# Five seven-product pairs per feed-forward unit, with the copies, sums and residual adds around them re-ordered

## The chip, the cores and the metric

The kernel runs on one core of one Trainium2 chip. The metric is the device time of one execution, in microseconds. Engines are named as in the profile: PE (TensorE) multiplies, DVE (VectorE) and ACT (ScalarE) work element by element, POOL (GpSimd) does a little of both and issues some transfers, SP (SyncE) issues the weight loads. TensorE writes to eight PSUM banks of 128 x 512 float32; everything else lies in SBUF.

## The reference

An encoder of two layers over 256 tokens, width 2048. Layer 0 mixes with grouped-query attention, layer 1 with a gated recurrence; after each mixer comes a feed-forward part, which is where the change lies:

```python
x = x + mixer(rms_norm(x, norm_mix[i]))
x = x + swiglu(rms_norm(x, norm_ffn[i]), w_gate[i], w_up[i], w_down[i])

def swiglu(h, w_gate, w_up, w_down):
    return (jax.nn.silu(h @ w_gate) * (h @ w_up)) @ w_down
```

w_gate and w_up are 2048 x 5632, w_down is 5632 x 2048. All inputs are float32.

## The kernel before

**Precision.** Each float32 operand is split into a high part (rounded to float32r, by a cast on ScalarE) and a low part (what is left, a subtraction on VectorE). One product of a 128 x 128 block of activations and a 128 x 512 block of weights is three matmuls: high x high, low x high, high x low (`product`, L291 to L297).

**Weights.** They stream in halves of 512 KB (1024 values per partition), in the order in which they are used. `load_half` (L119) issues the load on SP, casts on ACT (L127) and subtracts on DVE (L128). Raw halves have five buffers, split ones seven (`parts`, L108). `behind` (L114) chains all casts in program order, and all subtractions and sums of weights ("rest") in another chain, so on their engines these keep the order of the program. TensorE's order is the program's. Everything else on ACT, DVE and POOL is placed by a scheduler that goes through the program with a timeline of its own; within an engine instructions run in the order so fixed, and an instruction that waits holds back those behind it. `follow` adds one more constraint of order between two instructions.

**A feed-forward unit.** The 5632 hidden features are taken as 11 units of 512. A unit (L714) computes gate and up for its features and both halves of the tokens (a = 0, 1), over the 16 blocks of the input width in eight pairs c = 0 to 7. Four accumulators c11, c21 (gate) and c12, c22 (up) collect in PSUM. A plain pair takes two halves of weights and eight products, 24 matmuls. A seven-product pair treats the pair of blocks as a 2 x 2 matrix product by Strassen's scheme in Winograd's form and needs seven products, 21 matmuls. It pays for this with sums: `load_seven` (L136) forms four sums of weight blocks on DVE (L151, 128 x 512 each) and splits them too (L145 on ACT, L148 on DVE); the sums of activations ("forms") are made once per layer while the norm is turned (`form`, L425), one per pair that any unit computes in this way. Four more accumulators, m1, p5, p7, p6, serve these pairs. `SEVEN` (L30) names the pairs; `FEWER` (L31) gives fewer to units 0 to 2.

The seven products of a pair run in this order:

```python
(m1, a11, "b11"), (c11, a12, "b21"), (c12, n4, "b22"), (p5, n1, "t1"),
(p7, n3, "t3"), (p6, n2, "t2"), (c21, a22, "t4"),
```

**The end of a unit.** After its last seven-product pair: m1 is copied on ACT (L741), p6, p5, p7 and p5 again are added or subtracted on DVE (L742 to L745). After pair 7: c11 and c21 are added on DVE (L747), Silu on ACT, c12 and c22 subtracted from (L750), the products taken (L751). Then the 128 x 1024 result is transposed: DVE transposes 32 x 32 blocks (L376), sixteen ACT copies put them in place (L383), and the result is split again (L753, L754).

**Order of the work.** `ffn_plan` (L178): units 0 and 1, then each further unit followed by two of the four "down" groups of the part before it (one group: 512 output columns, 8 blocks of hidden features, four halves of weights, 48 matmuls), unit 10 without any; at the end the last part of 12 blocks (`groups`, L323). The four m1, p5, p7, p6 banks and the down groups' banks come from one pool of four ("pm"); c11 to c22 and the last part's banks from another pool of four ("acc"). Each down group's two banks are added to the residual x_tm (in SBUF) by `add_residual` (L314, the add is L317, on DVE).

Of the kernel before, what the change touches and what calls it, by code (L numbers as in the profile page):

```python
# [12 lines left out]
F32 = mybir.dt.float32  # L13
F32R = mybir.dt.float32r
AF = mybir.ActivationFunctionType
ALU = mybir.AluOpType
AX = mybir.AxisListType

P = 128
S = 256  # L20
# [6 lines left out]
DFF = 5632  # L27
PARTS = [8, 8, 8, 8, 12]
UNIT = 4
SEVEN = (0, 1, 3, 5)  # L30
FEWER = {0: (0, 3, 5), 1: (1, 5), 2: (1, 5)}  # L31
HALF = 8
CHUNK = HALF * P
WIDE = 512
# [38 lines left out]
def trunk(ctx, tc, w, out):  # L73
    nc = tc.nc
    act, dve, pool, pe, sync = nc.scalar, nc.vector, nc.gpsimd, nc.tensor, nc.sync
# [15 lines left out]
    def tmp(tag, shape=(P, S), dt=F32, bufs=2):  # L91
        pl = tp if tag in COMMON else scope[-1]
        return pl.tile(list(shape), dt, tag=tag, name=nm(tag), bufs=bufs)
# [4 lines left out]
    def follow(i, j):  # L98
        tc.add_manual_dep(
            i.ins, j.ins.name,  # L100
            mybir.DependencyInfo(mybir.DependencyClass.NoSync, mybir.DependencyReason.DATA),
            reason="order",
        )


    ring, held, ft = [0], [], []

    def parts(shape):  # L108
        n = ring[0] = (ring[0] + 1) % (RING + MORE)
# [4 lines left out]
    def behind(key, i):  # L114
        if key in newest:
            follow(i, newest[key])
        newest[key] = i

    def load_half(src, pieces=1, then=None):  # L119
        raw = wp.tile([P, CHUNK], F32, tag="raw", name=nm("raw"), bufs=RING)  # L120
# [15 lines left out]
    def load_seven(srcs):  # L136
        raw = [wp.tile([P, 2, WIDE], F32, tag="raw", name=nm("raw"), bufs=RING) for _ in range(2)]
        for r, src in zip(raw, srcs):
            sync.dma_start(out=r, in_=src)
        (b11, b21), (b12, b22) = ([r[:, j, :] for j in range(2)] for r in raw)  # L140
        got = {}

        def two(src, names):
            hi, lo = parts([P, 2, WIDE]) if len(names) > 1 else [tmp(t, (P, 1, WIDE), F32R) for t in ("ohi", "olo")]
            behind("cast", act.copy(hi, src))  # L145
            for j, name in enumerate(names):
                got[name] = hi[:, j, :], lo[:, j, :]
            return lambda: behind("rest", dve.tensor_tensor(lo, src, hi[:].bitcast(F32), ALU.subtract))  # L148

        def add(o, x, y):  # L150
            behind("rest", dve.tensor_tensor(o, x, y, ALU.add))  # L151

        sums = [tmp("ws", (P, 2, WIDE)) for _ in range(2)]
        (t1, t3), (t2, t4) = ([t[:, j, :] for j in range(2)] for t in sums)
        two(raw[0], ("b11", "b21"))()
        add(t1, b11, b12)
        add(t3, b12, b22)
        two(raw[1][:, 1:, :], ("b22",))()
        first = two(sums[0], ("t1", "t3"))
        add(t2, t1, b22)  # L160
        add(t4, t2, b21)
        second = two(sums[1], ("t2", "t4"))
        first()
        second()
        return got
# [21 lines left out]
    def ffn_order(l):  # L187
        seq = []
        for what, i in ffn_plan():
# [3 lines left out]
            both = [(w[f"w_gate{l}"][i, c], w[f"w_up{l}"][i, c]) for c in range(KT // 2)]  # L193
            seq += sum(([b] if c in (FEWER.get(i, SEVEN)) else list(b) for c, b in enumerate(both)), [])
        return seq + out_order(w[f"w_down{l}_{len(PARTS) - 1}"], UNIT // 2)
# [112 lines left out]
    def wide_project(xs, total, bank=new_acc):  # L308
        accs = [bank() for _ in range(2)]
        for k0 in range(0, total, 2):  # L310
            wide(accs, xs, k0, total)
        return accs

    def add_residual(g, accs, norm, store=False):  # L314
        for a in range(2):
            o = x_tm[:, a, g * WIDE : (g + 1) * WIDE]
            dve.tensor_tensor(o, o, accs[a], ALU.add)  # L317
            if store:
                sync.dma_start(out=out[:, a, g * WIDE : (g + 1) * WIDE], in_=o)
        if norm is not None:  # L320
            norm.add(g)
# [30 lines left out]
    x_tm = cst.tile([P, 2, D], F32, tag="x", name="x")  # L352
# [17 lines left out]
        return pk[:, o : o + 1]  # L370


    def turn_blocks(src, engines, own=None):
        turned = tmp("one", (P, 2, WIDE), bufs=1)
        own = tmp("two", (P, 2, WIDE), bufs=1) if own is None else own
        dve.transpose(turned, src)  # L376
        t = own.rearrange("p a (b c) -> p (a b) c", c=S)
        for i in range(4):
            of = turned[32 * i : 32 * i + 32].rearrange("p a (k j c) -> p k a j c", k=4, j=4)
            for j in range(4):  # L380
                to = t[32 * j : 32 * j + 32].rearrange("p k (a i c) -> p k a i c", a=2, i=4)
                eng = engines[(4 * i + j) % len(engines)]
                (eng.copy if eng is act else eng.tensor_copy)(to[:, :, :, i, :], of[:, :, :, j, :])  # L383
        return t

    class Norm:
# [30 lines left out]
        def turn(self, g, engines):  # L417
# [3 lines left out]
            for i in range(2):  # L421
                if self.g[0] == "norm_ffn" and 2 * g + i in SEVEN:
                    self.form(2 * g + i, t[:, 2 * i : 2 * i + 2, :])

        def form(self, c, src):  # L425
# [4 lines left out]
            for i, x, y, op in (  # L430
# [3 lines left out]
                pool.tensor_tensor(t[:, i, :], x, y, op)  # L434
            hi, lo = (tmp(f"f{n}", (P, 4, P), F32R, bufs=len(SEVEN)) for n in "hl")
            act.copy(hi, t)
# [227 lines left out]
    def act_four():  # L664
        return xp.tile([P, UNIT, 2 * S], F32R, tag="act", name=nm("act"), bufs=4)
# [44 lines left out]
    def ffn(norm, nxt):  # L710
        def bank():
            return ps_m.tile([P, 2 * S], F32, tag="pm", name=nm("pm"))

        def unit(seven):  # L714
            xs, r = norm.xs, [norm.r[:, a : a + 1] for a in range(2)]
            m1, p5, p7, p6 = (bank() for _ in range(4))
            c11, c21, c12, c22 = (new_acc() for _ in range(4))
            new = [m1, p5, p7, p6, c11, c21, c12, c22]

            def fresh(o):  # L720
                n = len(new)
                new[:] = [b for b in new if b is not o]
                return len(new) < n

            for c in range(KT // 2):
                if c not in seven:
                    for pair in ((c11, c21), (c12, c22)):
                        wide(pair, xs, 2 * c, KT, [fresh(o) for o in pair])
                    continue
                wt, end = half(), c == seven[-1]  # L730
                n1, n3, n2, n4 = norm.forms[c]
                a11, a12, a22 = block(xs, 2 * c, 0), block(xs, 2 * c + 1, 0), block(xs, 2 * c + 1, 1)
                for o, x, y in (
                    (m1, a11, "b11"), (c11, a12, "b21"), (c12, n4, "b22"), (p5, n1, "t1"),
                    (p7, n3, "t3"), (p6, n2, "t2"), (c21, a22, "t4"),
                ):
                    product(o, x, wt[y], fresh(o), end and any(o is m for m in (m1, p5, p7, p6)))
                if end:
                    one, h = (tmp(n, (P, 2, WIDE), bufs=1) for n in ("one", "two"))
                    (base, u), (v, x) = ([t[:, a, :] for a in range(2)] for t in (one, h))  # L740
                    act.copy(base, m1)  # L741
                    dve.tensor_tensor(u, base, p6, ALU.add)  # L742
                    dve.tensor_tensor(v, u, p5, ALU.subtract)
                    dve.tensor_tensor(u, u, p7, ALU.add)
                    dve.tensor_tensor(x, u, p5, ALU.subtract)  # L745
            for o, y, b in ((base, base, c11), (u, u, c21)):
                dve.tensor_tensor(o, y, b, ALU.add)  # L747
            for a, (o, y, b) in enumerate(((base, v, c12), (u, x, c22))):
                table_act(o, o, AF.Silu, scale=r[a])
                dve.tensor_tensor(y, b, y, ALU.subtract)  # L750
                dve.scalar_tensor_tensor(y, y, r[a], o, ALU.mult, ALU.mult)  # L751
            t, ht = act_four(), turn_blocks(h, (act,), h)
            act.copy(t[:, :, :S], ht)  # L753
            dve.tensor_tensor(t[:, :, S:], ht, t[:, :, :S].bitcast(F32), ALU.subtract)  # L754
            return [t[:, k, :] for k in range(UNIT)]

        hid = [[] for _ in PARTS]
        ends = np.cumsum(PARTS) // UNIT
        for what, i in ffn_plan():
            if what == "unit":  # L760
                hid[int(np.searchsorted(ends, i, "right"))] += unit(FEWER.get(i, SEVEN))
            else:
                add_residual(i[1], wide_project(hid[i[0]], PARTS[i[0]], bank), None)
        if nxt is not None:
            ln_exp_tables()
        groups(hid[-1], PARTS[-1], PARTS[-1] - UNIT, lambda: None, partial(add_residual, norm=nxt, store=nxt is None))
        scope.pop()
        ft.pop().close()
# [216 lines left out]
```

## Time and profile before

| What | Value |
|---|---|
| three runs, us | 1986.05 to 1988.11, median 1986.53 |
| the profiled execution's own time, us | 1986.03 |
| its span, first to last instruction, us | 1984.2 |
| TensorE's granted clock, mean | 0.999 |
| busy: PE / DVE / ACT / POOL, us | 1970.6 / 1674.4 / 1333.5 / 267.6 |
| feed-forward, units 3 and 4 (423.4 to 548.6), us | 125.2 |

Rows of groups read: line, engine, operation, output <- inputs, shapes, count | busy us, mean ns of one | idle time of the engine before them and what ended it. Rows of the timeline read: start us, duration us, engine, line, operation, operands, count (an "x2" row covers two instructions back to back), and in brackets the engine's idle time before it with what released it. Rows of waits read: who waited <- for whom: us in total, times, longest. Rows of one tile's instructions give the shortest, median and longest duration in ns. Rows of a window give its length and, for each engine, busy us and instructions; then clock, DMA share and GB/s. A matmul's duration is modelled and overlaps with the next one's, so its price is the distance from start to start.

### The profile page before, as it was taken

To read this page: it belongs to the slowest core of one execution; us is meant where nothing else is said; L and a number is where in the kernel's file an instruction comes from. 1 tells how busy PE (TensorE), PEld (TensorE's weight loads), DVE (VectorE), ACT (ScalarE), POOL (GpSimd) and SP (SyncE) were. 2 spreads that over 40 slices of the span, in tenths; PEclk is the share of its full clock that TensorE was granted. 3 is DMA by queue.
4 is the path that set the end of the run, shared out by engine and by line. 5 is a ranking of instruction groups with operands and counts; after the bars stand their busy time and mean duration, and the time that the engine had idled before them with its cause. 6 is when DMAs were issued, how large, how long until landed. Compare 5 with 4: busy or idle time off the path is not lost.

```text
span 1984.2 us, 27870 instructions
## 1 busy us (share of the span) xinstructions
PE 1970.6 (99%) x9892; PEld 1677.0 (85%) x9892; DVE 1674.4 (84%) x2204; ACT 1333.5 (67%) x2081; POOL 267.6 (13%) x323
## 2 busy tenths in 40 slices
PE   9999999999999999999999999999999999999999
PEld 8888887888888888888999998878888888888887
DVE  7878699889899898987788986897898898988983
ACT  7677577666656666567688886867666666666662
POOL 0443150000000000000456540510000000000000
PEclk9999999999999999999999999999999999999999
DMA  8534646646675556656566555555576456655663
GB/s 315 165 126 132 208 150 223 217 166 208 193 242 196 174 200 205 233 193 203 189 194 184 190 157 185 197 188 194 181 234 213 169 203 201 234 202 168 202 219 132
DMA packets 108571, 386.06 MB, mean 195 GB/s; under 512 B 12176, under 2 KB 12432, under 8 KB 108304
## 3 DMA queue, kind: packets, MB, share of 16 engines
q1 hardware_dynamic: 108288, 384.26, 58.5%
q8 instruction: 78, 1.28, 0.3%
q14 instruction: 61, 0.50, 0.1%
q10 hardware_dynamic: 144, 0.02, 0.0%
HBM read 382.13 MB, written 2.10 MB: 194 GB/s over the span
## 4 chain that ended last, share of the span: by engine, by line
PE 90%; DVE 4%; DMA 2%; ACT 1%; POOL 1%; issue 1%; SPq 0%; POOLq 0%; DVEq 0%; ACTq 0%
PE acc L293 16%; PE acc L294 16%; PE acc L296 16%; PE pm L296 9%; PE pm L293 9%; PE pm L294 9%; PE acc L273 3%; PE acc L274 3%; PE acc L275 3%; DVE lo L128 1%; PE acc L262 1%; PE pm L274 1%; PE pm L275 1%; PE pm L273 1%; POOL hb L547 1%
## 5 line engine op out<-in xcount | busy, mean ns | idle before, releaser
L128 DVE TENSOR_TENSOR lo<-raw,hi 128x1024 fp32r<-128x1024 f32 (+1 forms) x549 | 674.0, 1250 | 145.5 <-ACT hi L127 139.2
L127 ACT CAST hi<-raw 128x1024 fp32r<-128x1024 f32 (+1 forms) x549 | 563.0, 1048 | 261.7 <-PE acc L294 167.6
L293 PE MATMUL acc<-hi,xg 128*128 128x512 f32 x940 | 366.6, 390 | 3.8 <-DVE one L747 3.8
L296 PE MATMUL acc<-lo,xg 128*128 128x512 f32 x940 | 366.5, 390 | 0.0
L294 PE MATMUL acc<-hi,xg 128*128 128x512 f32 x940 | 366.3, 390 | 0.0
L145 ACT CAST hi<-ws 128x1024 fp32r<-128x1024 f32 x156 | 163.5, 1053 | 236.4 <-DVE ws L151 223.5
L293 PEld LDWEIGHTS acc<-hi,xg 128*128 128x128 f32 x940 | 176.9, 188 | 41.6 <-DVE one L747 4.6
L148 DVE TENSOR_TENSOR lo<-ws,hi 128x1024 fp32r<-128x1024 f32 x156 | 190.2, 1223 | 25.1 <-ACT hi L145 22.4
L294 PEld LDWEIGHTS acc<-hi,xg 128*128 128x128 f32 x940 | 176.9, 188 | 36.8
L296 PEld LDWEIGHTS acc<-lo,xg 128*128 128x128 f32 x940 | 176.7, 188 | 36.9
L293 PE MATMUL pm<-hi,act 128*128 128x512 f32 x512 | 199.2, 389 | 0.0
L294 PE MATMUL pm<-hi,act 128*128 128x512 f32 x512 | 199.2, 389 | 0.0
L296 PE MATMUL pm<-lo,act 128*128 128x512 f32 x512 | 199.2, 389 | 0.0
L383 ACT COPY two<-one 32x256 f32<-32x256 f32 x436 | 175.9, 403 | 12.9 <-DVE one L376 7.5
L293 PE MATMUL acc<-hi,act 128*128 128x512 f32 x448 | 174.6, 390 | 0.0
L296 PE MATMUL acc<-lo,act 128*128 128x512 f32 x448 | 174.4, 389 | 0.0
L294 PE MATMUL acc<-hi,act 128*128 128x512 f32 x448 | 174.3, 389 | 0.0
L383 POOL COPY two<-one 32x256 f32<-32x256 f32 x84 | 56.6, 673 | 785.9 <-ACT form L406 645.9
L273 PE MATMUL acc<-xg,hi 128*128 128x256 f32 x512 | 144.8, 283 | 0.0
L274 PE MATMUL acc<-xg,hi 128*128 128x256 f32 x512 | 144.6, 282 | 0.0
L275 PE MATMUL acc<-xg,lo 128*128 128x256 f32 x512 | 144.5, 282 | 0.0
L262 PE MATMUL acc<-xg,hi 128*128 128x512 f32 x384 | 125.6, 398 | 1.1 <-DVE xg L398 1.1
(217 smaller groups left out, 3678.6 us busy)
## 6 DMA issues: line engine op xcount, KB each, us to landing
raw<-in_w_gate_dram SPq DMA_DIRECT2D x176, 512.0 KB, 4.4
raw<-in_w_up_dram SPq DMA_DIRECT2D x176, 512.0 KB, 3.5
raw<-in_w_down_dram SPq DMA_DIRECT2D x176, 512.0 KB, 4.7
raw<-in_w_in_dram SPq DMA_DIRECT2D x64, 512.0 KB, 4.4
raw<-in_w_qv_dram SPq DMA_DIRECT2D x40, 512.0 KB, 3.8
raw<-in_w_o_dram SPq DMA_DIRECT2D x32, 512.0 KB, 3.5
raw<-in_w_out_dram SPq DMA_DIRECT2D x32, 512.0 KB, 3.6
graw<-in_w_gates_dram SPq DMA_DIRECT2D x32, 256.0 KB, 3.9
```

Of the source, the lines that this page charges most:

```text
L127: behind("cast", act.copy(hi[:, sl], raw[:, sl]))
L128: behind("rest", dve.tensor_tensor(lo[:, sl], raw[:, sl], hi[:, sl].bitcast(F32), ALU.subtract))
L145: behind("cast", act.copy(hi, src))
L148: return lambda: behind("rest", dve.tensor_tensor(lo, src, hi[:].bitcast(F32), ALU.subtract))
L262: pe.matmul(acc, w, xs[k], start=(k == 0), stop=stop)
L273: pe.matmul(o, hi, x[:, :S], start=start, stop=False)
L274: pe.matmul(o, hi, x[:, S:], start=False, stop=False)
L275: pe.matmul(o, lo, x[:, :S], start=False, stop=stop)
L293: pe.matmul(o, xh, wh, start=start, stop=False)
L294: pe.matmul(o, xl, wh, start=False, stop=False)
L296: pe.matmul(o, xh, wl, start=False, stop=stop)
L383: (eng.copy if eng is act else eng.tensor_copy)(to[:, :, :, i, :], of[:, :, :, j, :])
```

## The change

Five things, all in the feed-forward parts. The diff is whole but for its context.

- `SEVEN` gains pair 6, so units 3 to 10 compute five pairs with seven products; `FEWER` keeps three, two and two for units 0 to 2 but moves units 1 and 2 from pairs 1 and 5 to 3 and 5. A fifth form is made per layer.
- The unit's second, third and fourth pm bank are handed out in the order p6, p7, p5.
- The sixteen copies of a unit's turn (units 2 to 9) are cut into four moves of four copies. They wait in `tail`, and each of the next unit's `load_seven` calls takes one, after the cast of b22 and ahead of the first cast of sums; the copies join the chain of casts. The split of the turned result goes with the last move. Units 0 and 1 keep the block on ACT, unit 10 shares its copies between ACT and DVE.
- `ahead` holds rules [n, instruction]: the n-th "rest" instruction on DVE after the rule is made has to follow that instruction. They are made for L745 (n = 4), the second L747 (n = 3) and the second L750 (n = 4).
- The down groups' banks are no longer added on DVE: ACT copies each to a buffer (two of them, tag "form"), and a transfer issued by POOL adds it to x_tm.

```diff
-SEVEN = (0, 1, 3, 5)
-FEWER = {0: (0, 3, 5), 1: (1, 5), 2: (1, 5)}
+SEVEN = (0, 1, 3, 5, 6)
+FEWER = {0: (0, 3, 5), 1: (3, 5), 2: (3, 5)}
...
-    ring, held, ft = [0], [], []
+    ring, held, ft, ahead, tail = [0], [], [], [], []
...
         if key in newest:
             follow(i, newest[key])
         newest[key] = i
+        for rule in [rule for rule in ahead if key == "rest"]:
+            rule[0] -= 1
+            if rule[0] == 0:
+                follow(i, rule[1])
+                ahead.remove(rule)
...
         two(raw[1][:, 1:, :], ("b22",))()
+        if tail:
+            tail.pop(0)()
         first = two(sums[0], ("t1", "t3"))
...
-    def turn_blocks(src, engines, own=None):
+    def turn_blocks(src, engines, own=None, spread=None):
...
-        for i in range(4):
+
+        def move(i):
             of = turned[32 * i : 32 * i + 32].rearrange("p a (k j c) -> p k a j c", k=4, j=4)
             for j in range(4):
...
-                (eng.copy if eng is act else eng.tensor_copy)(to[:, :, :, i, :], of[:, :, :, j, :])
+                m = (eng.copy if eng is act else eng.tensor_copy)(to[:, :, :, i, :], of[:, :, :, j, :])
+                if spread is not None:
+                    behind("cast", m)
+
+        for i in range(4):
+            move(i) if spread is None else spread.append(partial(move, i))
         return t
...
-        def unit(seven):
+        def unit(seven, beside, engines):
...
-            m1, p5, p7, p6 = (bank() for _ in range(4))
+            m1, p6, p7, p5 = (bank() for _ in range(4))
...
-                    dve.tensor_tensor(x, u, p5, ALU.subtract)
+                    ahead.append([4, dve.tensor_tensor(x, u, p5, ALU.subtract)])
             for o, y, b in ((base, base, c11), (u, u, c21)):
-                dve.tensor_tensor(o, y, b, ALU.add)
+                features = dve.tensor_tensor(o, y, b, ALU.add)
             for a, (o, y, b) in enumerate(((base, v, c12), (u, x, c22))):
                 table_act(o, o, AF.Silu, scale=r[a])
-                dve.tensor_tensor(y, b, y, ALU.subtract)
+                last = dve.tensor_tensor(y, b, y, ALU.subtract)
                 dve.scalar_tensor_tensor(y, y, r[a], o, ALU.mult, ALU.mult)
-            t, ht = act_four(), turn_blocks(h, (act,), h)
-            act.copy(t[:, :, :S], ht)
-            dve.tensor_tensor(t[:, :, S:], ht, t[:, :, :S].bitcast(F32), ALU.subtract)
+            ahead.extend([[3, features], [4, last]])
+            t, ht = act_four(), turn_blocks(h, engines, h, tail if beside else None)
+
+            def parted(move=list):
+                move()
+                act.copy(t[:, :, :S], ht)
+                dve.tensor_tensor(t[:, :, S:], ht, t[:, :, :S].bitcast(F32), ALU.subtract)
+
+            if beside:
+                tail.append(partial(parted, tail.pop()))
+            else:
+                parted()
             return [t[:, k, :] for k in range(UNIT)]
...
-                hid[int(np.searchsorted(ends, i, "right"))] += unit(FEWER.get(i, SEVEN))
+                hid[int(np.searchsorted(ends, i, "right"))] += unit(FEWER.get(i, SEVEN), 1 < i < ends[-1] - 1, (act,) if i < ends[-1] - 1 else (act, dve))
             else:
-                add_residual(i[1], wide_project(hid[i[0]], PARTS[i[0]], bank), None)
+                for a, acc in enumerate(wide_project(hid[i[0]], PARTS[i[0]], bank)):
+                    t = tmp("form", (P, WIDE))
+                    act.copy(t, acc)
+                    pool.dma_start(out=x_tm[:, a, i[1] * WIDE : (i[1] + 1) * WIDE], in_=t, accum_op=ALU.add)
```

## The prediction

> **What bounds the kernel now.** I read the page's busy shares first, then the chain that ended last, then what TensorE waits for, then the stretches of the feed-forward stages on each engine.
>
> ```profile
> span 1984.2 us, 27870 instructions
> PE 1970.6 (99%) x9892; PEld 1677.0 (85%) x9892; DVE 1674.4 (84%) x2204; ACT 1333.5 (67%) x2081; POOL 267.6 (13%) x323
> PE 90%; DVE 4%; DMA 2%; ACT 1%; POOL 1%; issue 1%; SPq 0%; POOLq 0%; DVEq 0%; ACTq 0%
> PE acc L293 <- DVE one L747: 3.8, 2, 1.9
> 512.15:637.47 125.32, 125.32 (x554) 103.43 (x553) 111.85 (x128) 78.92 (x105) 0.00 (x0) 1.00 0.60 201
> 423.42 0.39 PE L293 MATMUL pm<-hi,xg 128*128 128x512 f32 x1
> ...
> 548.58 0.39 PE L293 MATMUL pm<-hi,xg 128*128 128x512 f32 x1
> ```
>
> TensorE is busy for all but 13.6 us of the span, at full clock, and 90% of the chain is its own work. The largest entry among its waits is 3.8 us, in two pieces. The window row covers two feed-forward units with the four down groups between: TensorE 100%, VectorE 111.85 of 125.32 (89%), ScalarE 63%. So matmuls set the time there, and VectorE is the engine that could take over.
>
> A matmul's 0.39 us isn't its price, because neighbours overlap. The last two rows are the first matmuls of units 3 and 5. Between them lie two units of 180 (four pairs of 21, four of 24) and four down groups of 48, 552 in all: 125.16 / 552 = 0.2267 us each.
>
> **Part 1, the fifth seven-product pair.** Units 3 to 10 of both layers compute pair 6 with 21 matmuls instead of 24; units 0 to 2 keep their number of short pairs. That is 2 x 8 x 3 = 48 matmuls, 48 x 0.2267 = 10.9 us off TensorE. The Trainium skill ("TensorE: Matmul & The Clock Gate", section "Back-to-back issue gap") gives about 131 ns as the sustained spacing at 512 columns; by it the gain would be 6.3 us. The trace's spacing differs from it and decides.
>
> The pair costs VectorE and ScalarE more:
>
> ```profile
> 617.78 1.22 DVE L148 TENSOR_TENSOR lo<-raw,hi 128x1024 fp32r<-128x1024 f32 x1
> ...
> 624.47 2.35 DVE L128 TENSOR_TENSOR lo<-raw,hi 128x1024 fp32r<-128x1024 f32 x2
> 626.74 1.22 DVE L148 TENSOR_TENSOR lo<-raw,hi 128x1024 fp32r<-128x1024 f32 x1
> L317 DVE TENSOR_TENSOR x<-x,pm 128x512 f32<-128x512 f32 x64 | 43.0, 683 | 39.9 <-PE pm L296 39.9
> L741 ACT COPY one<-pm 128x512 f32<-128x512 f32 x22 | 12.7, 575 | 0.0
> ACT hi L145 <- DVE ws L151: 223.5, 124, 3.7
> ```
>
> One seven-product pair occupies VectorE from 617.78 to 624.47, 6.69 us, a plain pair from 624.47 to 626.74, 2.27 us: +4.42 us per unit. ScalarE gains one and a half casts, about 1.5 us; it stands still for 223.5 us waiting for VectorE's sums, so that is covered.
>
> **Part 2, the residual.** Per unit four adds of 683 ns leave VectorE, 2.7 us, and with them 39.9 us of VectorE queue time spent waiting for TensorE. ScalarE gets four copies (as the 575 ns evacuation in L741: 2.3 us per unit, 64 in all) and POOL, idle in this stage, issues the transfers. VectorE's net per unit is +4.4 - 2.7 = +1.7 us, to 57.6 of 62.0 us, 93%. ScalarE goes from 39.5 to 43.3 us. Neither becomes the bound on the average.
>
> Averages don't settle it, so I follow VectorE's lead: how long a weight's low part is ready before the matmul that reads it.
>
> ```profile
> 552.26 2.49 DVE L148 TENSOR_TENSOR lo<-ws,hi 128x1024 fp32r<-128x1024 f32 x2
> ...
> 557.22 0.39 PE L296 MATMUL pm<-lo,fh 128*128 128x512 f32 x1
> 596.62 6.63 ACT L383 COPY two<-one 32x256 f32<-32x256 f32 x16
> 603.27 2.01 ACT L145 CAST hi<-ws 128x1024 fp32r<-128x1024 f32 x2
> ```
>
> Unit 5's second pair is finished at 554.75 and read at 557.22: 2.5 us, the smallest lead away from a stage's start. TensorE needs 12 x 0.2267 = 2.72 us for a half that VectorE makes in 1.14, so each plain half adds 1.58 us of lead; a seven-product pair takes 6.69 - 21 x 0.2267 = 1.93 us. One turn (a unit and two down groups) takes VectorE 55.9 us, half the window row: 16 halves (18.2), four pairs (26.8), the adds (2.7), and what is left, 8.2 us, is the unit's sums and transposing. In lead: +25.3 - 7.7 - 2.7 - 8.2 = +6.7 us to spare. After: 14 halves (+22.1), five pairs (-9.7) and the same sums, +4.2 us. Smaller, still positive, and the eight down halves in each turn (+12.6) refill it. The deepest run-down is two neighbouring pairs, -3.9, at pairs 0 and 1 and again at 5 and 6, with three halves' gain between. On that count TensorE doesn't starve.
>
> **Part 3, the turn's copies.** Today the sixteen copies stand in one block of 6.63 us, and the sums' casts behind it (603.27) come late. Now four at a time, 1.66 us, go between a pair's last raw cast and its first cast of sums, where ScalarE waits for VectorE anyway. I cost this at nothing, covered by the 223.5 us; if a copy stands there before VectorE has transposed, each such pair's lead shrinks by that delay. Unit 10's copies are shared with VectorE, 3.3 us earlier, ahead of 21.8 us of other projections: no effect.
>
> **Part 4, last sums ahead of later weights.** Where no down groups follow, the next unit wants its accumulator banks at once:
>
> ```profile
> 314.20 0.68 DVE L747 TENSOR_TENSOR one<-one,acc 128x512 f32<-128x512 f32 x1
> ...
> 316.00 1.22 DVE L148 TENSOR_TENSOR lo<-ws,hi 128x1024 fp32r<-128x1024 f32 x1
> 317.14 0.68 DVE L747 TENSOR_TENSOR one<-one,acc 128x512 f32<-128x512 f32 x1
> 317.87 0.50 PE L293 MATMUL acc<-hi,xg 128*128 128x512 f32 x1 [1.87 <-DVE one L747]
> 589.10 1.28 DVE L750 TENSOR_TENSOR two<-acc,two 128x512 f32<-128x512 f32 x2
> ```
>
> In unit 0 the second L747 stands behind weight work of unit 1's pair 1, and TensorE waits 1.87 us, once per layer. The change puts both L747 before the third later weight step and makes units 1 and 2 use pairs 3 and 5, so no such pair stands there: I take 3.4 of the 3.8 us as gained. Next late would be c12's bank, wanted 2.7 us later.
>
> What now queues behind these sums: the second, third and fourth half of the following down group wait for L745, L747 and L750 in turn. L750 runs as soon as the unit ends (589.10 to 590.38 in unit 5), the fourth half follows to 591.6, and TensorE reads it 8.6 us (three halves and two matmuls) after the unit's end at 548.58 + 180 x 0.2267 = 589.4, at 598.0: a lead of 6.4. Covered.
>
> **Part 5, the fifth form.** Its one VectorE and three ScalarE instructions per layer fall into unit 0's start, where nothing is spare:
>
> ```profile
> 291.73 1.22 DVE L148 TENSOR_TENSOR lo<-ws,hi 128x1024 fp32r<-128x1024 f32 x1
> 293.00 0.50 PE L296 MATMUL pm<-lo,fh 128*128 128x512 f32 x1
> L437 DVE TENSOR_TENSOR fl<-form,fh x8: 678/682/693, 248.1 to 1302.2; 128x512 fp32r<-128x512 f32 x8
> L428 ACT ACTIVATE form<-two,pk x16: 493/495/510, 243.4 to 1291.3; 128x256 f32<-128x256 f32 x16
> L436 ACT CAST fh<-form x8: 604/618/627, 247.4 to 1300.0; 128x512 fp32r<-128x512 f32 x8
> ```
>
> Low part done at 292.95, read at 293.00. Bounds: nothing, if the form is put after this stretch, or 0.68 + 2 x 0.495 + 0.62 = 2.3 us per layer if all of it pushes the chain. I take VectorE's 0.7, as VectorE is the engine without gaps there: +1.4 us.
>
> **Sum.** The profiled execution's own time is 1986.03 us: 1986.0 - 10.9 - 3.4 + 1.4, and +1.0 for small new stalls at unit borders (between 0 and the first two rivals' prices) gives 1974.1. The median shown, 1986.53, lies 0.5 above it, so 1974.6. The forecast's own range goes down to 1970 (form free, all 3.8 gained, no new stalls: 1971.8, less some 2 us out of TensorE's other 9.8 us of idle time, which a new order of the other engines can shift either way) and up to 1979 (nothing gained in part 4: 1978.0, and 1 us more of stalls).
>
> **Rival A, slower: the fourth bank comes late.** Down groups use the unit's four pm banks in order, so the second group's last bank is the next unit's fourth. That was p6, read in the sixth product; now it is p5, used in the fourth.
>
> ```profile
> 551.06 0.68 DVE L317 TENSOR_TENSOR x<-x,pm 128x512 f32<-128x512 f32 x1
> 551.98 0.39 PE L293 MATMUL pm<-hi,fh 128*128 128x512 f32 x1
> ```
>
> VectorE freed that bank at 551.74, 3.16 us after unit 5's start at 548.58; p6 wanted it at 551.98. Now it is wanted after nine matmuls, 2.04 us. If ScalarE empties it no earlier, TensorE stands 1.1 us in each of 16 units: 18 us, 1992.5. From 0.75 us late per unit (11.9 / 16) the whole gain is gone. For it: the lag in the trace, and copies behind a cast that waits. Against: two 575 ns copies fit into 2.04 us, and ScalarE has 30% spare.
>
> **Rival B, about even: VectorE's lead doesn't refill.** The new order makes VectorE stand still until p6 and c21 are complete. If it idles more than the 4.2 us to spare per turn, TensorE waits for the rest; half a microsecond in each of 16 turns is 8 us, 1982.6. For: lead of 2.5 before. Against: that came from the copy block and the adds in VectorE's queue, and both go.
>
> **Rival C, much slower: the transfers are slow.** Two buffers hold the copies, so a transfer must land before the next group's copy 10.9 us later.
>
> ```profile
> raw<-in_w_gate_dram SPq DMA_DIRECT2D x176, 512.0 KB, 4.4
> x<-in_xt_dram SPq DMA_DIRECT2D x1, 2048.0 KB, 12.0
> L434 POOL TENSOR_TENSOR form<-form x16: 462/773/1446, 244.1 to 1292.7; 128x128 f32<-128x128 f32 x16
> ```
>
> 256 KB read twice and written once is 768 KB; between the two load rows, my estimate is 6 us. At 12 us ScalarE waits about 1.5 us per unit, 24 us in all: 1998. For: POOL's adds stretch from 462 to 1446 ns beside a busy VectorE, and POOL must prepare the transfers. The Trainium skill ("SBUF — State Buffer", section "Who interferes with whom") says that VectorE's two-input operations contend with GpSimd's reads, and infers that preparing transfers, which writes, is spared; the POOL row fits the first half, and no row here shows the second.
>
> **Not what it says?** The pair counts can be read from the code; the 64 adds don't vanish but go to ScalarE.
>
> **Chances.** Forecast 0.66; A 0.13; B 0.12; C 0.05; anything else 0.04. About 0.2% (4 us) is what a measurement of this kernel can tell from no change, so faster means under 1982.6: all of the forecast, half of B, some of the rest, 0.75; same 0.10; slower 0.15. The range goes from 1970 to 1984: it takes in the forecast and most of B, and leaves out A and C.
>
> **What would show it.** Right: TensorE busy for about 1960 us with 48 matmuls fewer, units 3 to 10 coming every 62.0 us where down groups lie between, VectorE near 93% there, turn copies in fours between casts, and the two waits of 1.87 us gone. Wrong: waits of the matmul at p5 on ScalarE's copy (A), of matmuls on L148 inside units 3 to 10 (B), ScalarE waiting for transfers (C), or turns longer than 62.0 us with none of these. Unit 0's start shows whether the form costs 0.7 us per layer.

## The result and the profile after

The changed kernel takes 1975.76 us (median of 4 runs, 1975.56 to 1976.93), the kernel before beside it 1986.63 us (1986.05 to 1988.11). The ratio is 0.9945, 95% interval [0.9931, 0.9958]: faster by 10.9 us. The forecast was 1974.6, with a range of 1970 to 1984. The profiled execution took 1975.67 us of its own time.

The page after, for the lines shown of before:

```profile
span 1973.9 us, 28168 instructions
PE 1959.6 (99%) x9844; PEld 1667.3 (84%) x9844; DVE 1707.5 (87%) x2254; ACT 1389.0 (70%) x2167; POOL 329.2 (17%) x395
PE 86%; DVE 6%; ACT 3%; POOL 2%; issue 2%; DMA 1%; SPq 0%; ACTq 0%; POOLq 0%; DVEq 0%
```

TensorE issues 48 matmuls fewer (9844 against 9892) and is busy for 11.0 us less, and is still busy for all but 14.3 us: the bound is the same engine with less to do. Next, the first of TensorE's waits (total, times, longest):

```profile
PE pm L303 <- DVE lo L153: 2.6, 4, 0.8
```

A window over two feed-forward turns:

```profile
511.50:635.50 124.00, 124.00 (x549) 102.68 (x548) 115.30 (x133) 86.34 (x116) 6.94 (x8) 1.00 0.71 221
```

And the timeline: the first matmuls of units 3 and 5, then VectorE's last low part of unit 5's pair 6 and the matmul that reads it:

```profile
423.97 0.39 PE L300 MATMUL pm<-hi,xg 128*128 128x512 f32 x1
...
547.73 0.39 PE L300 MATMUL pm<-hi,xg 128*128 128x512 f32 x1
...
573.88 2.49 DVE L153 TENSOR_TENSOR lo<-ws,hi 128x1024 fp32r<-128x1024 f32 x2
...
581.50 0.39 PE L303 MATMUL pm<-lo,fh 128*128 128x512 f32 x1
```

The wait on L747 (3.8 us before) is gone, and waits on low parts have come, 2.6 us. Two turns take 547.73 - 423.97 = 123.76 us for 546 matmuls, the same 0.2267 us each. VectorE is busy for 115.30 of 124.00 us, 93%, ScalarE for 86.34, 43.2 us per turn. The low part read at 581.50 was ready at 576.37: a lead of 5.1 us, the smallest anywhere in units 3 to 10, where before it was 2.5.

To see where the time went I took the first matmul of each part in both traces and compared how far apart they lie:

| part | layer 0, us | layer 1, us |
|---|---|---|
| unit 0 | +1.5 | +1.1 |
| unit 1 | -0.9 | -2.7 |
| unit 2 | 0.0 | 0.0 |
| units 3 to 10 | -5.75 | -5.5 |
| last part and what follows | +1.25 (to layer 1's feed-forward) | +0.8 (to the end, stores included) |

With -0.1 ahead of unit 0 that is -10.3, the difference of the spans. Units 3 to 10 give 0.70 us each, which is all of the gain forecast for the fifth pair. Unit 0 has lost more than forecast, and unit 1 gained less than its old waits. Unit 0 in the timeline, with the rows of POOL, VectorE, ScalarE and TensorE that matter:

```profile
295.52 3.18 POOL L447 TENSOR_TENSOR form<-form 128x128 f32<-128x128 f32 x2 [9.48 <-ACT form L441]
...
297.49 0.88 DVE L153 TENSOR_TENSOR olo<-raw,ohi 128x512 fp32r<-128x512 f32 x1
...
298.77 1.33 POOL L447 TENSOR_TENSOR form<-form,form 128x128 f32<-128x128 f32 x2
...
300.13 0.62 ACT L449 CAST fh<-form 128x512 fp32r<-128x512 f32 x1 [4.36 <-POOL form L447]
...
300.79 0.69 DVE L450 TENSOR_TENSOR fl<-form,fh 128x512 fp32r<-128x512 f32 x1 [1.20 <-ACT fh L449]
...
303.27 0.51 PE L303 MATMUL pm<-lo,fh 128*128 128x512 f32 x1 [0.78 <-DVE lo L153]
```

The fifth form's cast stands in ScalarE's queue ahead of the next casts of weights and waits 4.36 us for POOL's four additions and subtractions. VectorE waits 1.20 us behind it, and TensorE comes late. What costs here is the wait in front of the form's cast, more than the instructions themselves.

The theory for the experiments: the time is the count of matmuls as long as VectorE's lead stays above zero; copies, sums and transfers matter by what they do to that lead. Rivals: the new order brings most of the gain by itself; the fifth pair needs no help; banks or transfers come late.

### The profile page after: what moved, and what is told of

It is laid out like the page before. It is cut to its first block, busy times and chain, and to the rows that moved or that the text cites. A ratio compares the mean times of both kernels' runs of the same rounds, so it can differ in the third digit from the quotient of the medians.

```text
span 1973.9 us, 28168 instructions
## 1 busy us (share of the span) xinstructions
PE 1959.6 (99%) x9844; PEld 1667.3 (84%) x9844; DVE 1707.5 (87%) x2254; ACT 1389.0 (70%) x2167; POOL 329.2 (17%) x395
## 4 chain that ended last, share of the span: by engine, by line
PE 86%; DVE 6%; ACT 3%; POOL 2%; issue 2%; DMA 1%; SPq 0%; ACTq 0%; POOLq 0%; DVEq 0%
PE acc L300 15%; PE acc L301 15%; PE acc L303 15%; PE pm L303 10%; PE pm L301 10%; PE pm L300 10%; PE acc L280 3%; PE acc L281 3%; PE acc L282 3%; DVE lo L133 2%; PE acc L269 1%; POOL hb L560 1%; PE pm L281 1%; PE pm L282 1%; PE pm L280 1%
## 5 line engine op out<-in xcount | busy, mean ns | idle before, releaser
L133 DVE TENSOR_TENSOR lo<-raw,hi 128x1024 fp32r<-128x1024 f32 (+1 forms) x517 | 631.5, 1251 | 85.6 <-ACT hi L132 84.7
L132 ACT CAST hi<-raw 128x1024 fp32r<-128x1024 f32 (+1 forms) x517 | 528.4, 1048 | 208.1 <-DMA raw<-in_w_down_dram 85.5
L300 PE MATMUL acc<-hi,xg 128*128 128x512 f32 x844 | 328.4, 389 | 0.0
L303 PE MATMUL acc<-lo,xg 128*128 128x512 f32 x844 | 328.4, 389 | 0.0
L301 PE MATMUL acc<-hi,xg 128*128 128x512 f32 x844 | 328.3, 389 | 0.0
L150 ACT CAST hi<-ws 128x1024 fp32r<-128x1024 f32 x188 | 197.9, 1053 | 152.2 <-DVE ws L156 131.7
L153 DVE TENSOR_TENSOR lo<-ws,hi 128x1024 fp32r<-128x1024 f32 x188 | 229.0, 1225 | 50.8 <-ACT hi L150 47.4
L788 POOL DMA_DIRECT2D x<-form x64 | 55.7, 919 | 1062.6 <-ACT form L787 1062.6
L301 PEld LDWEIGHTS acc<-hi,xg 128*128 128x128 f32 x844 | 158.4, 188 | 33.0
L303 PEld LDWEIGHTS acc<-lo,xg 128*128 128x128 f32 x844 | 158.4, 188 | 32.9
L300 PEld LDWEIGHTS acc<-hi,xg 128*128 128x128 f32 x844 | 158.4, 188 | 32.8
L156 DVE TENSOR_TENSOR ws<-ws,raw 128x512 f32<-128x512 f32 x188 | 129.7, 690 | 2.6
```

The lines of the kernel that those rows point to most:

```text
L132: behind("cast", act.copy(hi[:, sl], raw[:, sl]))
L133: behind("rest", dve.tensor_tensor(lo[:, sl], raw[:, sl], hi[:, sl].bitcast(F32), ALU.subtract))
L300: pe.matmul(o, xh, wh, start=start, stop=False)
L301: pe.matmul(o, xl, wh, start=False, stop=False)
L303: pe.matmul(o, xh, wl, start=False, stop=stop)
```

## The experiments

All medians are beside runs of the kernel before on the same chip; those lay at 1986.6 to 1987.4 us, so up to 0.8 us of a difference from the changed kernel's 1975.76 can come from the set of runs. A unit's excess is what it lasts, from first matmul to first matmul, beyond 0.2267 us for each of its matmuls.

**The fifth pair alone**, on the kernel before:

```diff
-SEVEN = (0, 1, 3, 5)
-FEWER = {0: (0, 3, 5), 1: (1, 5), 2: (1, 5)}
+SEVEN = (0, 1, 3, 5, 6)
+FEWER = {0: (0, 3, 5), 1: (3, 5), 2: (3, 5)}
```

> The kernel before with the fifth seven-product pair alone (new lists of pairs, nothing else). Theory (the time is the count of matmuls as long as VectorE's lead stays above zero; the other edits only keep that lead): VectorE keeps +1.5 us to spare per turn on paper (22.1 - 9.7 - 8.2 - 2.7), but the block of sixteen copies and the adds that wait in its queue stay, and they had taken the lead down to 2.4 us before; TensorE then waits for weights some tenths to 1 us per unit, so 1977 to 1988, I say 1981. Rival 1 (the other edits bring nothing): 1976, no wait of TensorE on weights in units 3 to 10. Rival 2 (the other edits bring most of it): 1986 or more.

Measured: 2021.78 us, ratio 1.0177 [1.0156, 1.0199]. The same 48 matmuls are gone, and the kernel is 34 us slower than before. TensorE's three largest entries among its waits:

```profile
PE pm L296 <- DVE lo L148: 17.3, 9, 2.3
PE acc L293 <- DVE one L747: 5.2, 3, 2.5
PE acc L293 <- DVE two L750: 3.8, 2, 2.5
```

A window over two turns:

```profile
659.90:781.00 121.10, 116.84 (x504) 95.07 (x503) 107.96 (x129) 73.48 (x99) 0.00 (x0) 0.99 0.54 183
```

And ScalarE's wait for the transposing, ahead of its copies:

```profile
ACT two L383 <- DVE one L376: 34.9, 16, 3.1
```

Eight of the sixteen units with five pairs last 1.4 to 5.2 us longer than their matmuls need, 33 us in all; units 0 and 1 together last 12 us longer. VectorE isn't full (108 of 121 us); its +1.5 us to spare on paper is lost in waits for ScalarE's late casts, since the copies wait in ScalarE's queue for the transposing (34.9 us, 7.5 before). My 1981 was far off: a budget of busy times says nothing about engines that wait for each other. The clock in this execution is 0.993 against 0.999, and the trace shows what that adds. Here is one of the waits in unit 6, two of the matmuls behind it, and a window over the stretch that follows:

```profile
625.25 0.50 PE L296 MATMUL pm<-lo,fh 128*128 128x512 f32 x1 [2.33 <-DVE lo L148]
...
627.18 0.63 PE L293 MATMUL acc<-hi,xg 128*128 128x512 f32 x1
627.60 0.63 PE L294 MATMUL acc<-hi,xg 128*128 128x512 f32 x1
```

```profile
626.72:630.13 3.41, 3.41 (x9) 2.64 (x8) 3.41 (x4) 1.84 (x3) 0.00 (x0) 0.50 0.62 219
```

For 3.41 us the granted clock was 0.50, and the matmuls start 0.43 us apart. Seven such stretches (one of 6.83 us) follow TensorE's waits of 1.8 to 2.5 us; three other waits as long have none behind them. Some 10 of the 45 us that the units lose are these slow matmuls, and nearly all of the rest is the waits and the steps next to them.

**Everything but the fifth pair:**

```diff
-SEVEN = (0, 1, 3, 5, 6)
+SEVEN = (0, 1, 3, 5)
```

> The changed kernel with four seven-product pairs (0, 1, 3, 5) in units 3 to 10, everything else as changed. Theory: 48 matmuls more are 48 x 0.2267 = 10.9 us, the fifth form's 2.6 us in unit 0 go away, so 1975.8 + 10.9 - 2.6 = 1984.1, about 2.5 below the kernel before. Rival (the new order is itself worth much, or the matmuls less): below 1981.

Measured: 1981.48 us, ratio 0.9972 [0.9961, 0.9983]. The order alone gives some 6 us: unit 1's excess over its matmuls falls from 2.2 and 3.9 us to 0.2 in both layers, and all other units are as before. The time is also 2.6 us less than I expected, since unit 1's stall of the changed kernel (1.3 and 1.2 us) is gone here along with unit 0's. Net, the fifth pair brings 5.7 us: 10.9 off the matmuls, about 5 given back in units 0 and 1.

**Adds of the residual on VectorE again:**

```diff
-                for a, acc in enumerate(wide_project(hid[i[0]], PARTS[i[0]], bank)):
-                    t = tmp("form", (P, WIDE))
-                    act.copy(t, acc)
-                    pool.dma_start(out=x_tm[...], in_=t, accum_op=ALU.add)
+                add_residual(i[1], wide_project(hid[i[0]], PARTS[i[0]], bank), None)
```

> The changed kernel with the down groups' adds back on VectorE instead of ScalarE's copy and a transfer. Theory of the late fourth bank: VectorE frees it about 3.1 us after the next unit's start, p5 wants it after 2.04 us, so TensorE waits about 1.1 us in each of 16 units: 1975.8 + 17.6 = 1993; if the lead had been the point (5.0 us less 2.7 per turn), TensorE would wait on low parts instead, or not at all and the time would stay within 1976 to 1978. What is looked for: a wait of the matmul on VectorE's add.

Measured: 1977.26 us, ratio 0.9954 [0.9939, 0.9968]: no loss of 1.1 us per unit, and no wait of a matmul on an add in the list of waits. A window, then the start of unit 6 in the timeline:

```profile
670.00:790.00 120.00, 120.00 (x531) 99.27 (x530) 115.61 (x136) 79.34 (x106) 0.00 (x0) 1.00 0.61 208
```

```profile
610.11 0.39 PE L300 MATMUL pm<-hi,xg 128*128 128x512 f32 x1
...
611.76 0.68 DVE L324 TENSOR_TENSOR x<-x,pm 128x512 f32<-128x512 f32 x1
...
612.14 0.39 PE L300 MATMUL pm<-hi,fh 128*128 128x512 f32 x1
...
612.96 0.68 DVE L324 TENSOR_TENSOR x<-x,pm 128x512 f32<-128x512 f32 x1
```

Unit 6 starts at 610.11 here; its fourth product, p5's, runs at 612.14, before the second add has even begun. So p5's bank isn't the one that the add frees. VectorE is at 96% and the lead goes down to 0.2 us in most units: the transfers buy 4.9 us of lead and, here, no more than 1.5 us of time.

**The copies of every unit in one block:**

```diff
-unit(..., 1 < i < ends[-1] - 1, (act,) if i < ends[-1] - 1 else (act, dve))
+unit(..., False, (act,) if i < ends[-1] - 1 else (act, dve))
```

> The changed kernel with the sixteen copies of every unit's turn in one block again (not cut into four moves). Theory: the block holds ScalarE 6.6 us, of which about 5 us come out of VectorE's lead; its smallest value in units 3 to 10 is 5.0 us, so it falls to about zero and TensorE waits up to 0.5 us per unit: 1976 to 1984, I say 1979. Rival (the cut is not needed): 1975.8, lead still above 2 us.

Measured: 1992.47 us, ratio 1.0025 [1.0014, 1.0036], 16.7 us above the changed kernel and slower than before. Two of TensorE's waits, then ScalarE and TensorE at the start of unit 6:

```profile
PE pm L303 <- DVE lo L153: 5.1, 14, 0.8
PE pm L300 <- ACT form L787: 4.3, 9, 1.0
```

```profile
607.71 2.89 ACT L391 COPY two<-one 32x256 f32<-32x256 f32 x7
610.63 2.00 ACT L150 CAST hi<-ws 128x1024 fp32r<-128x1024 f32 x2
...
614.17 0.39 PE L300 MATMUL pm<-hi,fh 128*128 128x512 f32 x1
...
614.95 1.06 ACT L787 COPY form<-pm 128x512 f32<-128x512 f32 x2
...
615.58 0.50 PE L300 MATMUL pm<-hi,fh 128*128 128x512 f32 x1 [0.57 <-ACT form L787]
```

From unit 6 on each unit lasts 0.9 to 1.8 us longer than its matmuls need. Two waits alternate. One is the low part, with the lead at zero, as expected. The other I hadn't expected here: the block pushes ScalarE's copies of the down group's banks back to 614.95, and the fifth product (p7) waits for the first copy. The fourth (p5) ran at 614.17, again ahead of the copies. The ten units lose 13.0 us in all; this execution also reached unit 0 2.2 us later than the changed kernel's, having had 3.41 us at a granted clock of 0.50 at 8.89.

**Without the rules for the last sums:**

```diff
-                    ahead.append([4, dve.tensor_tensor(x, u, p5, ALU.subtract)])
+                    dve.tensor_tensor(x, u, p5, ALU.subtract)
...
-            ahead.extend([[3, features], [4, last]])
```

> The changed kernel without the rules that put a unit's last sums ahead of later weights. Theory (the rules remove the wait of the next unit's accumulators on L747's sums, 1.87 us at unit 0's end in each layer, and matter nowhere else): the matmul after units 0 and 1 waits for the sums again, 2 to 4 us more in all, 1978 to 1980, and units 3 to 10 stay free of waits. Rival (the rules also keep the pm banks free for the down groups): waits of down matmuls on the sums, 1 us or more per unit, 1990 and above.

Measured: 1983.65 us, ratio 0.9987 [0.9977, 0.9996], 7.9 us above the changed kernel. The waits on L760's sums are back, all at the start of unit 1, and the last part now waits for the banks of unit 10's c12 and c22 (L763, 0.98 us in each layer):

```profile
PE acc L300 <- DVE one L760: 5.5, 3, 3.3
PE acc L300 <- DVE two L763: 2.0, 2, 1.0
```

Units 3 to 10 have no wait at all: the place was right but for the last part, the size too small, since unit 0 lost 1.6 and 3.8 us and unit 1 1.4 and 1.7 us more (in a profiled execution of 1988.2 us, the upper end of its runs). Some 4 us of this are matmuls that start 0.43 us apart, in stretches with a granted clock of 0.50 that begin at 321.74 and 1332.08, beside these waits.

**Banks handed out in the old order:**

```diff
-            m1, p6, p7, p5 = (bank() for _ in range(4))
+            m1, p5, p7, p6 = (bank() for _ in range(4))
```

> The changed kernel with the banks in the old order m1, p5, p7, p6. Theory: the first down group then takes p5's bank, which the last of four sums frees at about 3 us before the group's first matmul, and p6 comes fourth, wanted later than p5 would be, so nothing waits: 1975.8, within 1. Rival (the order is needed): first matmuls of down groups wait for L758, 0.5 to 2 us per unit, 1984 to 2000.

Measured: 1975.29 us, ratio 0.9942 [0.9927, 0.9957]: no difference. In the built programs the bank numbers of units and down groups are the same in both orders and in the kernel before: the order in which the code asks doesn't decide them, and p5 has the first down group's second bank, p6 the second group's last. The edit changes names only. But for these names the program is the changed kernel's, instruction for instruction, so this run measures the changed kernel a second time: 0.5 us apart by the medians, and 1.0 us between the profiled spans (1972.9 and 1973.9).

**The fifth form later** (its pair 6 isn't used before unit 3): its scaling goes behind unit 0's cast for pair 5, its split behind unit 2.

```diff
-                    self.form(2 * g + i, t[:, 2 * i : 2 * i + 2, :])
+                    now = partial(self.form, 2 * g + i, t[:, 2 * i : 2 * i + 2, :])
+                    if 2 * g + i == 6:
+                        self.late = partial(now, late=True)
+                    else:
+                        now()
...
+                if end and i == 0:
+                    norm.late()
...
+            if i == 2:
+                norm.late()
```

> The changed kernel with the fifth form (pair 6) made later: its scaling after unit 0's last cast of weights of pair 5, its split after unit 2. Theory (the form's cast stands in ScalarE's queue waiting for GpSimd's four adds, 4.4 us, and the late sums of unit 0 carry on into unit 1): unit 0 gets back 1.5 and 1.1 us, unit 1 about 1.1 and 1.0, 1971.1. Rival (unit 0's stall is the norm's small operations or the start of the stage, not the form): 1975.8, the wait of 0.8 us on the low part in unit 0 stays.

Measured: 1972.63 us, ratio 0.9929 [0.9914, 0.9944]. Unit 0's excess falls from 1.7 and 1.3 us to 0.2 and 0.0: the form is the cause there. Unit 1 keeps 1.5 and 0.7 us, so its stall isn't carried over from unit 0, and that half of my expectation failed.

**Copies of units 0 and 1 cut in two moves:**

```diff
-unit(..., 1 < i < ends[-1] - 1, (act,) if i < ends[-1] - 1 else (act, dve))
+unit(..., i < ends[-1] - 1, (act,) if i < ends[-1] - 1 else (act, dve))
...
             if beside:
                 tail.append(partial(parted, tail.pop()))
+                if i < 2:
+                    tail[:] = [lambda p=tail[n : n + 2]: [m() for m in p] for n in (0, 2)]
```

> The changed kernel with the turn's copies of units 0 and 1 cut as well, in two moves of eight copies at the next unit's two pairs. Theory (unit 1's stall at pair 3, 1.3 and 1.2 us, is the block of sixteen copies ahead of that pair's sums): the stall goes, 1973.3. Rival (it is VectorE's order or unit 0's lateness): unchanged, 1975.8, or more if the moves now come where ScalarE has no gap.

Measured: 1972.63 us, ratio 0.9928 [0.9914, 0.9943]. Unit 1's excess is zero in both layers. ScalarE in unit 1, first of the changed kernel, then with the copies cut:

```profile
328.82 6.63 ACT L391 COPY two<-one 32x256 f32<-32x256 f32 x16 [0.63 <-DVE one L383]
335.48 1.05 ACT L150 CAST hi<-ws 128x1024 fp32r<-128x1024 f32 x1
```

```profile
328.60 3.32 ACT L391 COPY two<-one 32x256 f32<-32x256 f32 x8 [5.78 <-DVE one L383]
331.95 2.00 ACT L150 CAST hi<-ws 128x1024 fp32r<-128x1024 f32 x2
```

The second cast of pair 3's sums, at 335.48 behind sixteen copies, comes at about 333 behind eight.

The block alone doesn't make this stall. With four pairs ("Everything but the fifth pair" above) it stands there too, and the low part behind it is ready 0.05 us before its matmul:

```profile
334.01 1.23 DVE L153 TENSOR_TENSOR lo<-ws,hi 128x1024 fp32r<-128x1024 f32 x1 [5.33 <-ACT hi L150]
...
335.29 0.50 PE L303 MATMUL pm<-lo,fh 128*128 128x512 f32 x1
```

In the changed kernel ScalarE casts one more half of weights ahead of Silu (the table load at 318.95), and waits for its transfer:

```profile
317.88 1.05 ACT L132 CAST hi<-raw 128x1024 fp32r<-128x1024 f32 x1 [1.22 <-DMA raw<-in_w_up_dram]
318.95 1.28 ACT L491 ACT_TABLE_LOAD   x1
```

The table load comes 2.4 us after the unit's first matmul, with four pairs 1.3 us after it. So in layer 0 the block takes all of the lead and this microsecond is what TensorE waits for. With the copies cut the table load is as late (2.3 us), and there is no stall.

**Both of these together:**

> The changed kernel with the late fifth form and with the copies of units 0 and 1 cut in two moves. Theory (two separate causes: the form costs unit 0 its 1.5 and 1.3 us, the block of copies costs unit 1 its 1.3 and 1.2 us): their gains add up, 1975.8 - 2.8 - 2.5 = 1970.5, and no wait of TensorE on a low part is left in either feed-forward stage. Rival (one cause that shows in one place or the other, as each alone gave the same time): about 1972.6 again, with a stall left in unit 0 or unit 1.

Measured: 1970.44 us, ratio 0.9920 [0.9907, 0.9934]. The gains add up (1972.63 and 1972.63 alone, 1970.5 expected), so there are two causes. No wait on a low part is left in the feed-forward stages, and this version beats both kernels. Its page begins:

```profile
span 1967.3 us, 28158 instructions
PE 1956.4 (99%) x9844; PEld 1667.4 (85%) x9844; DVE 1708.8 (87%) x2254; ACT 1387.4 (71%) x2167; POOL 327.7 (17%) x395
```

The matmuls are the same 9844; TensorE's time outside them is 10.9 us, against 14.3.

**A sixth pair:**

```diff
-SEVEN = (0, 1, 3, 5, 6)
+SEVEN = (0, 1, 3, 4, 5, 6)
...
-                if self.g[0] == "norm_ffn" and 2 * g + i in SEVEN:
+                if self.g[0] == "norm_ffn" and 2 * g + i in SEVEN and 2 * g + i != 4:
...
-                n1, n3, n2, n4 = norm.forms[c]
+                n1, n3, n2, n4 = norm.forms[3 if c == 4 else c]
```

> The changed kernel with a sixth seven-product pair (4) in units 3 to 10; the sums of activations of pair 3 stand in for those of pair 4, as a sixth form doesn't fit into SBUF, so the values of pair 4 are not the reference's. Theory (VectorE's budget: 12 halves give +19.0 us of lead per turn, six pairs take 11.6, the sums 8.2: 0.8 us short): TensorE saves 0.68 us per unit and waits 0.8 us and more, 1976 to 1980, waits on low parts in most of units 3 to 10. Rival (only the count of matmuls matters, VectorE still hides): 1975.8 - 10.9 = 1964.9 and a lead above zero.

Measured: 1984.5 us, ratio 0.9989 [0.9980, 0.9998]: 8.7 us above five pairs, with another 48 matmuls gone.

```profile
PE pm L303 <- DVE lo L153: 10.5, 16, 1.1
```

A window over two turns:

```profile
660.00:780.00 120.00, 118.29 (x519) 96.63 (x518) 117.65 (x140) 85.05 (x116) 6.96 (x8) 1.00 0.67 215
```

VectorE is at 98% (117.65 of 120.00) and now sets the time. Units 4 to 10 last 1.4 to 1.9 us longer than their matmuls, where the budget said 0.8; VectorE also waits for ScalarE's casts, which the budget leaves out.

## Why the prediction was right, point by point

- **The bound and the price of a matmul.** Right. 0.2267 us each after as before; units 3 to 10 gave 11.2 us where 10.9 was said. The figure of 131 ns from the Trainium skill ("TensorE: Matmul & The Clock Gate", "Back-to-back issue gap") would have made it 6.3; these matmuls don't follow it.
- **VectorE's and ScalarE's load.** Right: 93% and 43.2 us per turn, said 93% and 43.3. The lead stayed above zero (5.1 us) and the dip was where two pairs are neighbours, at pairs 5 and 6. But the budget worked only because the copies were cut: with the block VectorE is no busier (108.74 of 120.00 us) and TensorE stalls. Where I wrote "on that count TensorE doesn't starve", the count alone wasn't enough; the fifth pair alone and the block show it.

```profile
670.00:790.00 120.00, 119.01 (x521) 97.20 (x520) 108.74 (x126) 79.74 (x105) 5.21 (x6) 1.00 0.66 212
```

- **Residual by transfers.** In the feed-forward parts the transfers hide: POOL issues each in 0.86 us, they land after 4.8 us (3.3 to 8.1), said 6. But 0.7 us at the end of the span goes with them, which I had not counted: the span ends 4.85 us after its last matmul begins (1969.04 of 1973.9) in all versions with transfers, and 4.14 us after it in the three without (the kernel before, the fifth pair alone, the adds on VectorE). Their use was smaller than the rest of the change: 1.5 us.
- **The turn's copies, cost nothing.** Right as a cost. What the step was worth I didn't work out: 16.7 us by the medians, 13.0 of it in units 6 to 10.
- **Last sums ahead.** Said 3.4 us gained, measured 3.5 in unit 1; but that agreement is luck, as it is 6.1 us of old excess removed less 2.6 us of a new stall at pair 3. I had counted the two waits alone, 3.8 us. Before, the one in layer 1 (1.91 us, to 1329.13) was followed by 3.41 us at a granted clock of 0.50, from 1330.31, which is another 1.5 us; the rest lies in the steps next to the waits. I had named c12's bank as next late. It was the copies of unit 0, which I had left out of the step since the change doesn't touch them; moving unit 1's pair from 1 to 3 put its sums behind them.
- **The fifth form.** Said 1.4 us, with bounds of 0 and 4.6: 2.6 us, all of which the late form got back. I took VectorE's instruction for the cost; it was ScalarE's queue behind POOL.
- **New stalls elsewhere, +1.0.** 2.0 us outside the units, and none of it is a stall at a unit border, for which the term stood. Of the 0.8 us at the end, 0.7 goes with the transfers. The 1.25 us from layer 0's last part to layer 1's feed-forward isn't the change's: the run with the old bank names is the same program and takes 382.14 us there, as the kernel before does, against 383.39 in the changed kernel's execution. TensorE's list of waits has one of 0.8 us on L356 in the second and none in the first. So nothing that filled this term is what I had put it there for.
- **Rival A** rested on a misreading: banks aren't given out in the order of the code, so its price of 18 us could not arise in this way. Its mechanism, a product that waits for ScalarE's copy of a bank, did appear once the block was back. **Rival B** didn't occur with five pairs and did with six. **Rival C** didn't occur: with 8.1 us the slowest transfer stayed under 10.9.

The errors were +1.2 us in the form, +1.0 in other stalls, -0.5 in the matmuls and sums and -0.1 ahead of unit 0: the sum is 1.6 us below the profiled execution, the forecast 1.2 below the median.

## What to carry to other kernels

Removing work from the bound engine pays only while the helpers keep their lead, and the lead is a matter of what stands in front of what in an in-order queue: the same five pairs gave 34 us of loss without the new order (some 10 of it at the lower clock behind the waits) and 11 us of gain with it. So after a budget of busy times, look in each helper's queue for the longest run of instructions, and for any that waits for a third engine, ahead of something the bound engine needs; cut the run, or move it behind. And when a step moves one thing, check what it now stands behind, also where the diff touches nothing.

## What the runs showed of the hardware

After some of TensorE's waits the granted clock was 0.50 for 3.41 us or twice that: in the kernel before, behind 1.91 us (from 1330.31); with the fifth pair alone, behind seven of ten waits of 1.8 us or more. Product matmuls then start 0.43 us apart instead of 0.2267, so such a wait cost up to 1.6 us more than it lasted (8 slow steps in unit 6 there).

This row gives the shortest, median and longest time (ns) of half of POOL's 128 x 128 additions and subtractions:

```profile
L447 POOL TENSOR_TENSOR form<-form x20: 462/906/3182, 244.0 to 1304.9; 128x128 f32<-128x128 f32 x20
```

They took 462 ns at best and 3.18 us at most; in unit 0's rows above, two took 3.18 us while VectorE was busy throughout (3.18 of 3.18 us), and a VectorE subtraction of 0.69 us took 0.88 beside them. The Trainium skill ("SBUF — State Buffer", "Who interferes with whom") says that two-input operations of VectorE contend with GpSimd's reads; the rows agree. It infers that preparing transfers is spared. The instructions on the copies' buffers (shortest, median and longest ns), then the transfers on the page (KB each, us to landing):

```profile
L787 ACT COPY form<-pm x64: 587/588/592, 413.0 to 1864.1; 128x512 f32<-128x512 f32 x64
L788 POOL DMA_DIRECT2D x<-form x64: 852/862/1199, 413.9 to 1865.0; - x64
```

```profile
x<-form POOLq DMA_DIRECT2D x64, 256.0 KB, 4.8
```

The 64 issues took 852 to 1199 ns beside a VectorE that was busy for 93% of the time, which fits; no run here has them beside an idle VectorE.
